# The MLP's down projection as seven Strassen products, interleaved with the gate and value products

## The chip, the cores and the metric

The kernel runs on one core of one Trainium2 chip. The metric is the device time of one execution in microseconds (us). TensorE (PE) does the matmuls, VectorE (DVE), ScalarE (ACT) and GpSimd (POOL) the work on tiles; SyncE (SP) issues most DMA transfers.

## The reference

One encoder layer over 512 tokens of 2048 features, in float32: a normalisation, an input projection, a gating unit on half of the channels and a long convolution on the other half, an output projection, and then the part that matters here, a gated MLP with 5504 hidden channels, and a final normalisation.

```
h = rms_norm(x, norm2_g[l])
gv = h @ ffn_w_up[l]
g = dwconv3(gv[..., :D_FF], ffn_dw_w[l], ffn_dw_b[l])     # three taps along the tokens
val = gv[..., D_FF:]
x = x + (jax.nn.gelu(g, approximate=False) * val) @ ffn_w_down[l]
return rms_norm(x, final_g)
```

## The kernel before

A float32 product is computed as three products in a shorter format (`mm3`): each operand is split into `hi` (a rounded copy) and `lo` (the rest), and hi·hi, lo·hi and hi·lo are summed in PSUM. Weights stream in *units* of 128x1024 (512 KB): `plan` lists them in the order of use, `load_raw` issues the load on SP's queue into one of three buffers `raw`, ACT casts it to `hi`, DVE subtracts to get `lo` (`exact_pair`), and `next_unit` keeps splits two units and loads three units ahead of the matmuls. So the order of `plan` sets the order of the work on all engines; there is no scheduler that changes it.

Activations are kept as [feature, token]: `h2H`/`h2L` are the split, normalised activations of 16 blocks of 128 features, `xacc` the residual. In the gate and value products weights are stationary and 512 tokens move through; the profile's names give the moving tile first (`pa<-h2H,hi`).

The 5504 hidden channels are 43 blocks of 128: ten groups of four and a last group of three. The order is: gate of a group (8 units of 24 matmuls), down of the group before (8 units, 192 matmuls, `pd`), value of the group (8 units). When a gate is done, DVE multiplies its four PSUM banks by the norm's row (`ev`, L563), ACT and DVE compute the three taps (`cv`, L567 and two multiply-adds of L574 per block), ACT the GELU, GpSimd multiplies by the row again (`gg`, L1034). When a value is done, DVE multiplies (L1048) and the result is split into `aH`/`aL`. Each finished feature block of the down product is added to `xacc` (L1071). The weights of the last group's down product are all split ahead into `lH`/`lL`; that product (`pl`, 288 matmuls with 256 tokens) ends the kernel in two halves of the tokens, each followed by its normalisation: squares, ones-matmuls for the sum over features, a power on GpSimd, a row broadcast by TensorE, and scaled outputs. The output leaves as [feature, token] and is transposed by the host.

Tiles stand in SBUF one after another in the order in which they are declared. Three small pads (`pad`) shift what follows them.

Of the kernel before, what the change touches and what calls it, by code (L numbers as in the profile page):

```python
# [31 lines left out]
NCC = CB // CC  # L32

# [9 lines left out]
def encoder_kernel(ctx: ExitStack, tc: tile.TileContext, a: dict, out: bass.AP):  # L43
# [40 lines left out]
    def plan_down(gi):  # L84
        j0, nf = groups[gi]
        for q in range(4):
            plan.extend((w_dn, j0 + k0, min(2, nf - k0), q * 512, 512) for k0 in range(0, nf, 2))

    ffn_order = []
    for gi in range(last):  # L90
        ffn_order.append(("gate", gi))
        if gi:
            ffn_order.append(("down", gi - 1))
        ffn_order.append(("value", gi))
    ffn_order += [("gate", last), ("value", last), ("down", last - 1)]
# [8 lines left out]

    on_pool = set()
# [3 lines left out]
    for kind, gi in ffn_order:  # L109
        if kind == "down":  # L110
            plan_down(gi)
        else:
            plan_proj(w_up, (0 if kind == "gate" else DFF) + groups[gi][0] * P, groups[gi][1])

    raws, split_units = {}, {}
    st_ = {"dma": 0, "split": 0, "use": 0}
# [16 lines left out]

    def dma_to(n):
        while st_["dma"] < min(n, len(plan)):
            raws[st_["dma"]] = load_raw(plan[st_["dma"]])
            st_["dma"] += 1

    def split_to(n):
        while st_["split"] < min(n, len(plan)):  # L140
            i = st_["split"]
            dma_to(i + 1)
            _, _, nk, _, n_ = plan[i]
            raw = raws.pop(i)
            hi = wp.tile([P, 2, 512], F32R, tag="hi", name="hi", bufs=3)
            lo = wp.tile([P, 2, 512], F32R, tag="lo", name="lo", bufs=3)
            if i == 0:
                for k in range(nk):
                    exact_pair(hi[:, k, :n_], lo[:, k, :n_], raw[:, k, :n_])
            else:  # L150
                eng = POOL if i in on_pool else DVE
                exact_pair(hi[:, :nk, :n_], lo[:, :nk, :n_], raw[:, :nk, :n_], eng)
            split_units[i] = (hi, lo)
            st_["split"] += 1

    def next_unit(key):
# [506 lines left out]
    pad("padu", 128, stack=left)  # L663
# [21 lines left out]
    def sgu_pieces():  # L685
# [328 lines left out]
    act, gates = {}, {}  # L1014
    turn_ = [1]

    def four(name, n=4):
        turn_[0] += 1
        return [(bank, sbank)[turn_[0] % 2](name) for _ in range(n)]


# [4 lines left out]
    def gate(gi):  # L1026
        j0, nf = groups[gi]

        def take(ps):
            gg = []  # L1030
            for f, cv in conv3(ff, ps, r2[0], fw, j0):
                g_ = ff.tile([P, L], F32, tag="gg", name="gg", bufs=5)
                ACT.activation(g_, cv, AF.Gelu)  # L1033
                POOL.tensor_tensor(g_, g_, r2[0], ALU.mult)  # L1034
                gg.append(g_)
            gates[gi] = gg

        return projA(w_up, j0 * P, nf, take, hk)

    def value(gi):  # L1040
        j0, nf = groups[gi]

        def take(ps):
            aH = ff.tile([P, 4, L], F32R, tag="aH", name="aH", bufs=2)
            aL = ff.tile([P, 4, L], F32R, tag="aL", name="aL", bufs=2)
            gg = gates.pop(gi)
            for f, o in enumerate(ps):
                DVE.tensor_tensor(gg[f], gg[f], o, ALU.mult)  # L1048
            for f in range(nf):
# [5 lines left out]
    def down(gi):
        j0, nf = groups[gi]
        aH, aL = act.pop(gi)
        for q in range(4):
            ps = four("pd")
            for k0 in range(0, nf, 2):  # L1060
                nk = min(2, nf - k0)
                hi, lo = next_unit((w_dn, j0 + k0, nk, q * 512, 512))
                for kk in range(nk):
                    k = k0 + kk
                    for f in range(4):
                        fs_ = slice(f * P, (f + 1) * P)
                        mm3(ps[f], hi[:, kk, fs_], lo[:, kk, fs_], aH[:, k, :], aL[:, k, :], k == 0, k == nf - 1)
                if k0 + nk == nf:
                    for f, o in enumerate(ps):
                        x_ = xacc[:, 4 * q + f, :]  # L1070
                        DVE.tensor_tensor(x_, x_, o, ALU.add)  # L1071
                yield


    r2 = []
    for kind, gi in ffn_order:
        if kind == "gate":
            g = gate(gi)
            if gi == 0:
                for n, _ in enumerate(g):  # L1080
                    if n == 1:
                        norm2(3)
                    if n == 9:
                        r2c = rms_col(ss2s[0], D, "r2c")
                    if n == 11:
                        r2.append(row_of(r2c, "r2"))
            else:
                drain(g)
        elif kind == "value":
            drain(value(gi))  # L1090
        elif gi < last - 1:
            drain(down(gi))
# [8 lines left out]
    lL = lp_.tile([P, nf, D], F32R, name="lL")  # L1101

    def last_weights():
        for q in range(4):
            for k0 in range(0, nf, 2):
                nk = min(2, nf - k0)
                raw = load_raw((w_dn, j0 + k0, nk, q * 512, 512))
                cs = slice(q * 512, (q + 1) * 512)
                exact_pair(lH[:, k0 : k0 + nk, cs], lL[:, k0 : k0 + nk, cs], raw[:, :nk, :])
                yield  # L1110

    lw = last_weights()
    for _ in down(last - 1):
        next(lw, None)
    drain(lw)
    aH, aL = act.pop(last)
    ov = out.rearrange("(k p) t -> p k t", p=P)
    HW = L // 2
    def scale(d, hs, row, eng):
        x_ = xacc[:, d, hs]  # L1120
        if eng is POOL:
            ACT.activation(x_, x_, AF.Copy, scale=col("final", d))
            POOL.tensor_tensor(x_, x_, row[:, :HW], ALU.mult)
        else:
            DVE.scalar_tensor_tensor(x_, x_, col("final", d), row[:, :HW], ALU.mult, ALU.mult)  # L1125
        if d < 2 or d % 2:
            e = d if d < 2 else d - 1
            SP.dma_start(ov[:, e : d + 1, hs], xacc[:, e : d + 1, hs])

    nt = HW // P  # L1130

    def rms3():

        ms_ = [sbank("ms") for _ in range(nt)]

        def add(sq, first, final):
            for t in range(nt):
                PE.matmul(
                    ms_[t][:, 0:1], sq[:, t * P : (t + 1) * P], ones[:, 0:1], start=first, stop=final
                )  # L1140

        def close():
            r = const.tile([P, NT], F32, tag="rc", name="r3c", bufs=3)
            for t in range(nt):
                DVE.tensor_scalar(r[:, t : t + 1], ms_[t][:, 0:1], 1.0 / D, EPS, ALU.mult, ALU.add)
            POOL.tensor_tensor(r[:, :nt], r[:, :nt], nhalf.broadcast_to([P, nt]), ALU.pow)
            return r

        return add, close

    for th in range(2):
        hs = slice(th * HW, (th + 1) * HW)

        accs = [lp_.tile([P, HW], F32, tag=f"ss{i}", name=f"ss{i}", bufs=2) for i in range(2)]
        sqs = []
        for d in range(KD):
            if th and d == KD - 1:
                add, close = rms3()
                add(accs[0], True, False)
                add(accs[1], False, False)  # L1160
                add(sqs.pop(0), False, False)
# [17 lines left out]
            if th and d == 4:  # L1179
                row = row_of(r3c, "r3", nt)  # L1180
# [97 lines left out]
```

## Time and profile before

| | |
|---|---|
| median of 3 runs | 2146.39 us (2145.21 to 2148.4) |
| profiled execution | 2145.88 us |
| its span | 2144.1 us |
| TensorE busy | 2117.5 us (99%) |
| VectorE busy | 1117.2 us (52%) |
| ScalarE busy | 671.7 us (31%) |
| GpSimd busy | 219.5 us (10%) |
| matmuls (recorded) | 9734 |

Busy shares are means over the span, and a busy engine need not be at its best pace. What a matmul costs is therefore read from the distance between the starts of two that follow one another, not from the duration in its row, in which neighbours overlap.

### The profile page before, as it was taken

Reading aid. Unit: us, or ns where it says so; the run is one execution under the profiler, and the core shown is the slowest. Engines: PE = TensorE matmul, PEld = TensorE weight load, DVE = VectorE, ACT = ScalarE, POOL = GpSimd, SP = SyncE. Lnnn points to the kernel's source line nnn. Section 1 sums busy time; section 2 is a strip of 40 time slices with the busy share of each in tenths; the row PEclk is TensorE's granted clock in tenths of the full one; section 3 lists DMA queues with packets and bytes.
Section 4 is the critical chain, followed back from the end, with each engine's and each line's share of the span. In section 5 each row is a group of like instructions: output and inputs, shape, how many; then the busy total and the mean of one; then the engine's idle time right before and its main releaser. Section 6 shows DMA issues by size and latency. Waiting matters only on the chain.

```text
span 2144.1 us, 23726 instructions
## 1 busy us (share of the span) xinstructions
PE 2117.5 (99%) x9734; PEld 1761.1 (82%) x9734; DVE 1117.2 (52%) x1336; ACT 671.7 (31%) x851; POOL 219.5 (10%) x147
## 2 busy tenths in 40 slices
PE   8999999999999999999999999999999999999997
PEld 6888888888888888888888888888888888888887
DVE  6872675447888744435343363533635345353455
ACT  6443542223543323222221222212222122222233
POOL 0330310100004410001010010100101000010004
PEclk9999999999999999999999999999999999999998
DMA  8434233333233333333333333333333333332332
GB/s 290 142 117 134 80 88 98 99 120 126 84 104 128 118 91 96 99 99 98 89 98 100 97 99 99 98 98 94 94 98 98 98 94 103 94 94 86 104 115 79
DMA packets 114632, 227.29 MB, mean 106 GB/s; under 512 B 7163, under 2 KB 18619, under 8 KB 112732
## 3 DMA queue, kind: packets, MB, share of 16 engines
q1 hardware_dynamic: 109184, 215.69, 32.6%
q10 hardware_dynamic: 5340, 10.10, 1.4%
q8 instruction: 76, 1.25, 0.3%
q14 instruction: 32, 0.26, 0.0%
HBM read 217.37 MB, written 8.39 MB: 105 GB/s over the span
## 4 chain that ended last, share of the span: by engine, by line
PE 90%; DVE 6%; ACT 1%; issue 1%; DMA 1%; POOL 0%; ACTq 0%; SPq 0%; DVEq 0%
PE pa L172 19%; PE pa L170 19%; PE pa L171 19%; PE pd L171 7%; PE pd L172 7%; PE pd L170 7%; PE po L171 2%; PE po L172 2%; PE po L170 2%; PE pv L170 1%; PE pv L172 1%; PE pv L171 1%; DVE ev L561 1%; DVE lo L132 1%; DVE xacc L1125 1%
## 5 line engine op out<-in xcount | busy, mean ns | idle before, releaser
L132 DVE TENSOR_TENSOR lo<-raw,hi 128x1024 fp32r<-128x1024 f32 (+2 forms) x369 | 459.4, 1247 | 842.4 <-ACT hi L131 837.1
L131 ACT CAST hi<-raw 128x1024 fp32r<-128x1024 f32 (+2 forms) x369 | 382.5, 1037 | 1097.0 <-PE pa L171 708.5
L170 PE MATMUL pa<-h2H,hi 128*128 128x512 f32 x1376 | 535.6, 389 | 0.0
L172 PE MATMUL pa<-h2H,lo 128*128 128x512 f32 x1376 | 535.4, 389 | 0.0
L171 PE MATMUL pa<-h2L,hi 128*128 128x512 f32 x1376 | 535.4, 389 | 0.0
L171 PEld LDWEIGHTS pa<-h2L,hi 128*128 128x128 f32 x1376 | 258.4, 188 | 53.6
L172 PEld LDWEIGHTS pa<-h2H,lo 128*128 128x128 f32 x1376 | 258.4, 188 | 53.6
L170 PEld LDWEIGHTS pa<-h2H,hi 128*128 128x128 f32 x1376 | 258.4, 188 | 53.4
L172 PE MATMUL pd<-aH,lo 128*128 128x512 f32 x640 | 249.0, 389 | 0.0
L170 PE MATMUL pd<-aH,hi 128*128 128x512 f32 x640 | 249.0, 389 | 0.0
L171 PE MATMUL pd<-aL,hi 128*128 128x512 f32 x640 | 249.0, 389 | 0.0
L170 PE MATMUL pa<-hH,hi 128*128 128x512 f32 x512 | 202.4, 395 | 2.6 <-DVE ev L561 1.5
L172 PE MATMUL pa<-hH,lo 128*128 128x512 f32 x512 | 200.3, 392 | 1.4 <-DVE lo L132 1.4
L171 PE MATMUL pa<-hL,hi 128*128 128x512 f32 x512 | 200.5, 392 | 0.0
L1034 POOL TENSOR_TENSOR gg<-gg,r 128x512 f32<-128x512 f32 x43 | 73.0, 1700 | 1203.2 <-ACT gg L1033 1203.2
L170 PEld LDWEIGHTS pd<-aH,hi 128*128 128x128 f32 x640 | 120.2, 188 | 25.0
L172 PEld LDWEIGHTS pd<-aH,lo 128*128 128x128 f32 x640 | 120.2, 188 | 24.9
L171 PEld LDWEIGHTS pd<-aL,hi 128*128 128x128 f32 x640 | 120.2, 188 | 24.9
L1071 DVE TENSOR_TENSOR xacc<-xacc,pd 128x512 f32<-128x512 f32 x160 | 106.0, 683 | 39.9 <-PE pd L172 39.9
L170 PEld LDWEIGHTS pa<-hH,hi 128*128 128x128 f32 x512 | 96.8, 189 | 28.5 <-DVE ev L561 4.6
L172 PEld LDWEIGHTS pa<-hH,lo 128*128 128x128 f32 x512 | 96.6, 189 | 23.1 <-DVE lo L132 2.7
L171 PEld LDWEIGHTS pa<-hL,hi 128*128 128x128 f32 x512 | 96.8, 189 | 19.0
(241 smaller groups left out, 2157.0 us busy)
## 6 DMA issues: line engine op xcount, KB each, us to landing
raw<-in_ffn_w_up SPq DMA_DIRECT2D x160, 512.0 KB, 3.7
raw<-in_ffn_w_down SPq DMA_DIRECT2D x84, 512.0 KB, 3.6
raw<-in_w_in SPq DMA_DIRECT2D x79, 512.0 KB, 3.7
raw<-in_w_out SPq DMA_DIRECT2D x32, 512.0 KB, 3.7
raw<-in_ffn_w_up SPq DMA_DIRECT2D x16, 384.0 KB, 3.2
xn<-in_xN ACTq DMA_DIRECT2D x8, 512.0 KB, 4.8
khat_d<-kh SPq DMA_DIRECT2D x4, 1024.0 KB, 4.4
kh<-khat_d SPq DMA_DIRECT2D x4, 1024.0 KB, 4.8
```

The lines of the kernel that those rows point to most:

```text
L131: ACT.copy(hi, src)
L132: eng.tensor_tensor(lo, src, f32(hi), ALU.subtract)
L170: PE.matmul(o, ah, bh, start=start, stop=False)
L171: PE.matmul(o, ah, bl, start=False, stop=False)
L172: PE.matmul(o, al, bh, start=False, stop=stop)
L561: DVE.tensor_tensor(eo(e), pairs(o), pairs(r), ALU.mult)
L1034: POOL.tensor_tensor(g_, g_, r2[0], ALU.mult)
L1071: DVE.tensor_tensor(x_, x_, o, ALU.add)
L1125: DVE.scalar_tensor_tensor(x_, x_, col("final", d), row[:, :HW], ALU.mult, ALU.mult)
```

## The change

The down product of a group is computed by a scheme of Strassen's with seven products of half size in place of eight. The group's activations (512 hidden channels by 512 tokens) and each half of the output columns are cut into quarters; sums and differences of the quarters are formed on DVE, for the weights in place in their load buffers (`sraw`, 4 buffers), for the activations in three pieces per group (`operands`). A unit S0 to S13 is one of seven products for one of two column halves: 12 matmuls (`sa`, `se`, `sc`, `sg` by PSUM chain), in which now the weights move and the activations are stationary. Chains are read by DVE while they are still being summed (`read=True`), since several outputs contain the same partial sums (`shared` collects one of them over all groups).

The units are spread: G0 G1 G2 S0 G3 S1 G4 S2 G5 S3 G6 S4 G7 S5 S6 V0 S7 V1 S8 V2 S9 V3 S10 V4 S11 V5 V6 V7 S12 S13, where G and V are the gate and value units of a group and S those of the group before. The conv's work on a finished gate is cut into one piece per unit (`piece`), results are taken from PSUM behind the next unit's preparation (`flush`, `posts`).

`xacc` is turned to [token, feature] on TensorE during the first gate (`turn_x`, 16 blocks of four 128x128 transposes). The last group is 144 matmuls with 512 columns, and each of four token tiles is normalised by itself: ACT squares and sums a row, DVE multiplies by `grow` (final_g broadcast by a 1 MB load), and ACT and DVE scale; outputs leave on SP's and ACT's queues.

```diff
+SUMS = (
+    ("11", None, None), ("12", "12", "11"), ("22", None, None), ("22", "22", "12"),
+    ("11", "22", "11"), ("21", None, None), ("21", "21", "22"),
+)
...
+    for gi in range(len(groups)):
+        S = [("S", gi - 1, i // 7, i % 7) for i in range(14)] if gi else []
+        G, V = ([("R", kind, gi, k0) for k0 in range(0, KD, 2)] for kind in ("gate", "value"))
+        ffn_order += G[:3]
+        for i in range(5):
+            ffn_order += S[i : i + 1] + G[3 + i : 4 + i]
+        ffn_order += S[5:7]
+        late = 2 if gi == last else 0
+        for i in range(5 - late):
+            ffn_order += V[i : i + 1] + S[7 + i : 8 + i]
+        ffn_order += V[5 - late :] + S[12 - late :]
+    ffn_order += [("L", k0, q) for q in range(4) for k0 in range(0, groups[last][1], 2)]
...
+                into, of, less = SUMS[u]
+                raws[i] = sraws[gi, dp, into]
+                if of:
+                    DVE.tensor_tensor(raws[i], sraws[gi, dp, of], sraws[gi, dp, less], ALU.subtract)
...
+    def conv_piece(gi, f):
+
+        w0, w1, w2_, b = (col(*n(groups[gi][0] + f)) for n in fw)
+        e, d = gg[gi][:, f, :], tmp[f % 2]
+        ACT.activation(d, e, AF.Identity, bias=b, scale=w1)
+        DVE.scalar_tensor_tensor(d[:, 1:L], e[:, : L - 1], w0, d[:, 1:L], ALU.mult, ALU.add)
+        DVE.scalar_tensor_tensor(d[:, : L - 1], e[:, 1:L], w2_, d[:, : L - 1], ALU.mult, ALU.add)
+        ACT.activation(e, d, AF.Gelu)
+        POOL.tensor_tensor(e, e, r2[0], ALU.mult)
...
+    CHAIN = "aeeacgc"
...
+    def down_out(gi, dp, u, tp):
+        o = chains[dp, CHAIN[u]][tp]
+        if u == 3:
+            sh = shared[:, tp, dp, :]
...
+        else:
+            t, q = ((tp, dp), (tp + 2, dp + 2), (tp, dp + 2), None, (tp + 2, dp + 2), (tp, dp), (tp + 2, dp))[u]
+            add_to(t, q, as_out(o))
...
+        hi, lo = next_unit(e, flush)
+        for tp in range(2):
+            ts_ = slice(tp * P, (tp + 1) * P)
+            for k in range(2):
+                mm3(
+                    chains[dp, CHAIN[u]][tp], H[:, u, k, ts_], Lo[:, u, k, ts_], hi[:, k, :], lo[:, k, :],
+                    k == 0 and u not in (2, 3, 6), k == 1, True,
+                )
+            posts.append(lambda tp=tp: down_out(gi, dp, u, tp))
...
+    ssf = const.tile([P, NT, 4], F32, name="ssf")
...
+        o = ps_of.pop(("last", t, q))
+        x_ = fin[t][q]
+        DVE.tensor_tensor(as_out(x_), out_tile(t, q), as_out(o), ALU.add)
+        ACT.activation(tmp[q % 2], x_, AF.Square, accum_out=ssf[:, t, q : q + 1])
+        DVE.tensor_tensor(x_, x_, grow[0][:, q * 512 : (q + 1) * 512], ALU.mult)
...
+            if q % 2:
+                ACT.activation(x_, x_, AF.Copy, scale=r[:, 0:1])
+            else:
+                DVE.tensor_scalar(x_, x_, r[:, 0:1], None, ALU.mult)
+            (ACT if q % 2 else SP).dma_start(out[t * P : (t + 1) * P, q * 512 : (q + 1) * 512], x_)
```

Two of the three pads go (`padu`, 128 B, and `pady`, 384 B), and the new tile `ssf` (64 B) stands among the first. This moves the tiles on the left side of SBUF; those on the right stay. Start addresses in the two built programs, modulo 256 bytes:

| tiles | before | after |
|---|---|---|
| `hi`, `lo` (weights) | 128 | 192 |
| `hH`, `hL`, `h2H`, `h2L` (activations of the input, gate and value products) | 128 | 128 |
| `yh`, `ylo` (output projection, first half) | 128 | 192 |
| `ybH`, `ybL` (output projection, second half) | 0 | 192 |
| `aH`, `aL` (activations of the down product) | 128 | 192 |
| `lH`, `lL` and the last group's activations | 128 | 128 |

How the order on VectorE changes where a gate ends, inside the MLP. Before (`ev` are the gate's banks times the row, `cv` the conv, `lo` the splits, `xacc` the down product's sums):

```order
L563 TENSOR_TENSOR ev<-pa,r_5817 128x512 x3
L574 SCALAR_TENSOR_TENSOR cv<-ev,cols,cv 128x511
L563 TENSOR_TENSOR ev<-pa,r_5817 128x512
L574 SCALAR_TENSOR_TENSOR cv<-ev,cols,cv 128x511 x2
L132 TENSOR_TENSOR lo<-raw,hi 128x1024
L574 SCALAR_TENSOR_TENSOR cv<-ev,cols,cv 128x511 x5
L132 TENSOR_TENSOR lo<-raw,hi 128x1024
L1071 TENSOR_TENSOR xacc<-xacc,pd 128x512 x4
```

After (`gg` stands for `ev`, `tmp` for `cv`; `sg` and `sc` are Strassen chains; `lo<-sraw` splits a Strassen unit, `lo<-raw` a value unit):

```order
L1118 TENSOR_TENSOR gg<-pa,r_5854 128x512 x3
L1110 SCALAR_TENSOR_TENSOR tmp_5856<-gg,cols,tmp_5856 128x511
L1118 TENSOR_TENSOR gg<-pa,r_5854 128x512
L144 TENSOR_TENSOR lo<-raw,hi 128x1024
L1111 SCALAR_TENSOR_TENSOR tmp_5856<-gg,cols,tmp_5856 128x511
L1192 TENSOR_TENSOR xacc<-xacc,sg 128x4x128 x2
L144 TENSOR_TENSOR lo<-sraw,hi 128x1024
L1110 SCALAR_TENSOR_TENSOR tmp_5857<-gg,cols,tmp_5857 128x511
L1192 TENSOR_TENSOR xacc<-xacc,sc 128x4x128
L1111 SCALAR_TENSOR_TENSOR tmp_5857<-gg,cols,tmp_5857 128x511
L1192 TENSOR_TENSOR xacc<-xacc,sc 128x4x128
L144 TENSOR_TENSOR lo<-raw,hi 128x1024
```

All eight multiply-adds of the conv stood with one split between them; now they are spread over four units, with splits and sums of Strassen chains between.

The order on VectorE where the last group begins, behind the last value product. Before (`aL` splits the last group's activations, `lL` its weights, `lo` and `xacc` belong to the down product before it):

```order
L1048 TENSOR_TENSOR gg<-gg,pa 128x512 x3
L132 TENSOR_TENSOR aL<-gg,aH 128x512
L132 TENSOR_TENSOR lo<-raw,hi 128x1024
L132 TENSOR_TENSOR aL<-gg,aH 128x512 x2
L132 TENSOR_TENSOR lL<-raw,lH 128x2x512
L132 TENSOR_TENSOR lo<-raw,hi 128x1024
L132 TENSOR_TENSOR lL<-raw,lH 128x512
L1071 TENSOR_TENSOR xacc<-xacc,pd 128x512 x4
L132 TENSOR_TENSOR lo<-raw,hi 128x1024
L132 TENSOR_TENSOR lL<-raw,lH 128x2x512
L132 TENSOR_TENSOR lo<-raw,hi 128x1024
L132 TENSOR_TENSOR lL<-raw,lH 128x512
```

After (`laL` the last group's activations, `shared` the collected sums, `lL` the split weights, `fin` the outputs):

```order
L144 TENSOR_TENSOR laL<-gg,laH 128x512 x3
L144 TENSOR_TENSOR lo<-sraw,hi 128x1024
L1192 TENSOR_TENSOR xacc<-xacc,shared 128x4x128
L1192 TENSOR_TENSOR xacc<-xacc,sc 128x4x128 x2
L144 TENSOR_TENSOR lL<-raw,lH 128x2x512
L1192 TENSOR_TENSOR xacc<-xacc,shared 128x4x128
L1192 TENSOR_TENSOR xacc<-xacc,sg 128x4x128 x2
L144 TENSOR_TENSOR lL<-raw,lH 128x512
L1192 TENSOR_TENSOR xacc<-xacc,shared 128x4x128
L1192 TENSOR_TENSOR xacc<-xacc,sc 128x4x128 x2
L144 TENSOR_TENSOR lL<-raw,lH 128x2x512
L1192 TENSOR_TENSOR xacc<-xacc,shared 128x4x128 x3
```

The splits of the last group's weights, which before were spread over the down product ahead of it, stand among the last Strassen sums now.

## Rows read from the trace of the kernel before

**Rows 1.** The page: busy time by engine; TensorE's clock in 40 slices.
```profile
PE 2117.5 (99%) x9734; PEld 1761.1 (82%) x9734; DVE 1117.2 (52%) x1336; ACT 671.7 (31%) x851; POOL 219.5 (10%) x147
...
PEclk9999999999999999999999999999999999999998
```
**Rows 2.** Windows in the MLP: PE, PEld, DVE, ACT, POOL busy; PE clock; DMA.
```profile
1100.00:1600.00 500.00, 500.00 (x2208) 414.18 (x2207) 218.64 (x236) 126.34 (x141) 27.28 (x16) 1.00 0.33 97
1110.00:1122.00 12.00, 12.00 (x55) 9.94 (x54) 11.93 (x13) 6.96 (x10) 5.25 (x4) 1.00 0.14 44
```
**Rows 3.** Timeline of TensorE (start, duration): into the last group, and its end.
```profile
2088.85 0.39 PE L172 MATMUL pd<-aH,lo 128*128 128x512 f32 x1
2089.08 0.28 PE L170 MATMUL pl<-aH,lH 128*128 128x256 f32 x1
...
2127.63 0.42 PE L172 MATMUL pl<-aH,lL 128*128 128x256 f32 x1
```
**Rows 4.** Timeline of TensorE around a block of eight transposes.
```profile
498.09 1.04 PE L832 MATMUL ut<-ident,u 128*128 128x128 f32 x8
498.89 0.47 PE L170 MATMUL po<-yh,hi 128*128 128x512 f32 x1
499.20 0.39 PE L171 MATMUL po<-ylo,hi 128*128 128x512 f32 x1
...
500.82 0.40 PE L172 MATMUL po<-yh,lo 128*128 128x512 f32 x1
```
**Rows 5.** Timeline of TensorE: two stretches of seven matmuls, first and eighth of each.
```profile
660.54 0.39 PE L170 MATMUL po<-ybH,hi 128*128 128x512 f32 x1
...
662.17 0.39 PE L171 MATMUL po<-ybL,hi 128*128 128x512 f32 x1
...
1200.09 0.39 PE L172 MATMUL pa<-h2H,lo 128*128 128x512 f32 x1
...
1201.68 0.39 PE L170 MATMUL pa<-h2H,hi 128*128 128x512 f32 x1
```
**Rows 6.** Groups by line and form: count, busy us, mean ns of one, idle before.
```profile
L170 PE MATMUL pa<-h2H,hi 128*128 128x512 f32 x1376 | 535.6, 389 | 0.0
...
L132 DVE TENSOR_TENSOR lo<-raw,hi 128x1024 fp32r<-128x1024 f32 x351 | 442.3, 1262 | 804.9 <-ACT hi L131 799.6 <-PE mr L251 5.2
...
L1071 DVE TENSOR_TENSOR xacc<-xacc,pd 128x512 f32<-128x512 f32 x160 | 106.0, 683 | 39.9 <-PE pd L172 39.9
...
L170 PE MATMUL pa<-hH,hi 128*128 128x512 f32 x512 | 202.4, 395 | 2.6 <-DVE ev L561 1.5 <-ACT hi L131 1.0
...
L172 PE MATMUL pa<-hH,lo 128*128 128x512 f32 x512 | 200.3, 392 | 1.4 <-DVE lo L132 1.4
...
L170 PE MATMUL po<-ybH,hi 128*128 128x512 f32 x128 | 50.6, 395 | 0.0
...
L131 ACT CAST aH<-gg 128x512 fp32r<-128x512 f32 x43 | 25.6, 618 | 37.2 <-DVE gg L1048 36.6
...
L860 DVE TENSOR_TENSOR U<-G,kh 128x1024 f32<-128x1024 f32 x4 | 4.9, 1217 | 0.0
```
**Rows 7.** Timeline behind the last matmul: GpSimd's power, VectorE's scaling.
```profile
2130.68 0.71 POOL L1146 TENSOR_TENSOR r3c<-r3c,nhalf 128x2 f32<-128x2 f32 x1 [5.95 <-DVE r3c L1145]
...
2133.10 6.87 DVE L1125 SCALAR_TENSOR_TENSOR xacc<-xacc,cols,r 128x256 f32<-128x256 f32 x11 [2.50 <-ACT r L253]
```
**Rows 8.** Timeline of VectorE behind a gate: the conv's multiply-adds.
```profile
1111.27 1.40 DVE L574 SCALAR_TENSOR_TENSOR cv<-ev,cols,cv 128x511 f32<-128x511 f32 x2
...
1113.72 6.94 DVE L574 SCALAR_TENSOR_TENSOR cv<-ev,cols,cv 128x511 f32<-128x511 f32 x5
```
**Rows 9.** Timeline of GpSimd and VectorE at 702 us.
```profile
701.47 3.87 POOL L261 TENSOR_TENSOR ss<-ss,sq 128x512 f32<-128x512 f32 x2
...
701.86 2.31 DVE L132 TENSOR_TENSOR lo<-raw,hi 128x1024 fp32r<-128x1024 f32 x1
```
**Rows 10.** DMA issues by line: count, KB each, us to landing.
```profile
raw<-in_ffn_w_down SPq DMA_DIRECT2D x84, 512.0 KB, 3.6
```

More of the change, by code (lines that the diff above doesn't have):

```diff
@@ L108, in encoder_kernel @@
             plan.extend((w_out, half * 8 + k0, 2, q * 512, 512) for k0 in range(0, 8, 2))
-    for kind, gi in ffn_order:
-        if kind == "down":
-            plan_down(gi)
+    for e in ffn_order:
+        if e[0] == "R":
+            _, kind, gi, k0 = e
+            j0, nf = groups[gi]
+            plan.append((w_up, k0, 2, (0 if kind == "gate" else DFF) + j0 * P, nf * P))
         else:
-            plan_proj(w_up, (0 if kind == "gate" else DFF) + groups[gi][0] * P, groups[gi][1])
+            plan.append(e)
     raws, split_units = {}, {}
-    st_ = {"dma": 0, "split": 0, "use": 0}
+    st_ = {"dma": 0, "pre": 0, "split": 0, "use": 0}
     def load_raw(key):
@@ L661, in encoder_kernel @@
     fs.close()
-    pad("padu", 128, stack=left)
     yps.append(pool("y", stack=left))
@@ L1013, in encoder_kernel, with flush, piece @@
     fw = (lambda i: ("fw", i), lambda i: ("fw", NFF + i), lambda i: ("fw", 2 * NFF + i), lambda i: ("fb", i))
[L1014 to L1019, printed above, removed]
+    r2, sets = [], {}
+    shared = ff.tile([P, 2, 2, 512], F32, name="shared")
+    special["raw"] = lambda: ff.tile([P, 2, 512], F32, tag="sraw", name="sraw", bufs=4)
+    posts, pieces = [], []
+    def flush():
+        while posts:
+            posts.pop(0)()
+    def piece():
+        if pieces:
+            pieces.pop(0)()
     def hk(k):
@@ L1055, in down @@
[L1055 to L1072, printed above, removed]
@@ L1075, in encoder_kernel, with out_tile @@
[L1075 to L1078, printed above, removed]
-            if gi == 0:
[L1080 to L1086, printed above, removed]
-            else:
[L1088 to L1092, printed above, removed]
+    def out_tile(t, q):
+        return xacc[:, 4 * q : 4 * q + 4, t * P : (t + 1) * P]
@@ new lines, in gate_out, with value_out @@
+    def gate_out(gi):
+        gg[gi] = ff.tile([P, 4, L], F32, tag="gg", name="gg", bufs=1)
+        for f, o in enumerate(ps_of.pop(("gate", gi))):
+            DVE.tensor_tensor(gg[gi][:, f, :], o, r2[0], ALU.mult)
+            pieces.append(lambda f=f: conv_piece(gi, f))
+    def value_out(gi):
+        assert not pieces
+        g = gg[gi]
+        for f, o in enumerate(ps_of.pop(("value", gi))):
+            DVE.tensor_tensor(g[:, f, :], g[:, f, :], o, ALU.mult)
+        if gi < last:
+            pieces.extend(operands(gi))
@@ new lines, in regular @@
+    def regular(e, hook=None):
+        _, kind, gi, k0 = e
+        j0, nf = groups[gi]
+        if k0 == 0:
+            new = sbank if kind == "value" and gi == 0 else bank
+            ps_of[kind, gi] = [new("pa") for _ in range(nf)]
+        ps = ps_of[kind, gi]
+        hi, lo = next_unit((w_up, k0, 2, (0 if kind == "gate" else DFF) + j0 * P, nf * P), flush)
+        for kk in range(2):
+            k = k0 + kk
+            for f in range(nf):
+                fs_ = slice(f * P, (f + 1) * P)
+                mm3(ps[f], hi[:, kk, fs_], lo[:, kk, fs_], *hk(k), k == 0, k == KD - 1)
+            if hook:
+                hook(k)
+        if k0 == KD - 2:
+            posts.append(lambda: (gate_out if kind == "gate" else value_out)(gi))
@@ new lines, in first_hook @@
+    def first_hook(k):
+        if k == 0:
+            norm2(3)
+        if k == 8:
+            rows.append(rms_col(ss2s[0], D, "r2c"))
+        if k == 10:
+            r2.append(row_of(rows[0], "r2"))
+            tmp.append(const.tile([P, L], F32, tag="acc", name="tmp0", bufs=1))
+            tmp.append(const.tile([P, L], F32, tag="rb", name="tmp1", bufs=2))
+        for j in (k - 1, 15 if k == 15 else -1):
+            if j >= 0:
+                turn_x(j)
+    rows = []
+    units = iter(ffn_order)
@@ L1096, in encoder_kernel @@
+    for e in units:
+        if e[0] == "S":
+            strassen(e)
+        else:
+            regular(e, first_hook if e[1:3] == ("gate", 0) else None)
+        piece()
+        if e == ("R", "value", last, KD - 2):
+            break
     a2s.close()
@@ L1101, in encoder_kernel @@
     lL = lp_.tile([P, nf, D], F32R, name="lL")
-    def last_weights():
-        for q in range(4):
[L1105 to L1149, printed above, removed]
@@ L1185, in encoder_kernel, with last_pair @@
-    for i, sq in enumerate(sqs):
-        add(sq, False, i == len(sqs) - 1)
-    r3c = close()
-    row = row_of(r3c, "r3", HW // P)
-    for d in range(KD):
-        scale(d, slice(HW, L), row, POOL if d % 3 == 2 else DVE)
+    aH = lp_.tile([P, nf, L], F32R, name="laH")
+    aL = lp_.tile([P, nf, L], F32R, name="laL")
+    ssf = const.tile([P, NT, 4], F32, name="ssf")
+    def last_pair(k0, q):
+        nk = min(2, nf - k0)
+        cs = slice(q * 512, (q + 1) * 512)
+        return lH[:, k0 : k0 + nk, cs], lL[:, k0 : k0 + nk, cs], nk
@@ new lines, in encoder_kernel, with last_operands @@
+    special["last"] = last_pair
+    def last_operands():
+        g = gg.pop(last)
+        for f in range(nf):
+            exact_pair(aH[:, f, :], aL[:, f, :], g[:, f, :])
+        grow.append(ff.tile([P, D], F32, tag="gg", name="grow", bufs=1))
+        SP.dma_start(grow[0], a["final_g"].partition_broadcast(P))
+    grow, fin = [], {}
+    for e in units:
+        if e[0] == "L":
+            break
+        strassen(e)
+        if "last" in special and e == ("S", last - 1, 1, 4):
+            last_operands()
+        piece()
@@ new lines, in last_out @@
+    def last_out(t, q):
+        if q == 0:
+            if t < 2:
+                w = ff.tile([P, D], F32, tag=("aH", "aL")[t], name="fin", bufs=1)
+                fin[t] = [w[:, i * 512 : (i + 1) * 512] for i in range(4)]
+            else:
+                ws = [special["raw"]() for _ in range(2)]
+                fin[t] = [ws[i // 2][:, i % 2, :] for i in range(4)]
+        o = ps_of.pop(("last", t, q))
[3 more added lines that the diff above has]
+        DVE.tensor_tensor(x_, x_, grow[0][:, q * 512 : (q + 1) * 512], ALU.mult)
@@ new lines, in encoder_kernel @@
+    for q in range(4):
+        for k0 in range(0, nf, 2):
+            next_unit(("L", k0, q), flush)
+            while pieces:
+                piece()
+            for k in range(k0, min(k0 + 2, nf)):
+                for t in range(2):
+                    last_mm(t, q, k)
+        posts.extend(lambda t=t, q=q: last_out(t, q) for t in range(2))
+    for t in range(2, NT):
+        for q in range(4):
+            for k in range(nf):
+                last_mm(t, q, k)
+            flush()
+            last_out(t, q)
+            if t == 2 and q % 2:
+                leave(q // 2)
+            elif t == 3 and q == 1:
+                leave(2)
@@ L1191, in encoder_kernel @@
+    leave(3)
     tail.close()
```

206 lines of the change are left out of this document (121 added, 85 removed).

## The prediction

> **What bounds the kernel now.** I read the page first: TensorE is busy for 2117.5 of 2144.1 us, at the upper of its two clock levels in nearly every slice, VectorE for 1117.2 [rows 1]. Then the windows: between 1100 and 1600 us, inside the gated MLP, TensorE is busy for all 500.00 us with 2208 matmuls, and in the twelve microseconds in which VectorE has the least room (11.93 of 12.00 busy, GpSimd 5.25) it still starts 55 [rows 2]. So the MLP costs its matmuls and nothing else: 500.00/2208 = 0.2264 us for one of N=512. Last I read the timeline where a product changes shape and behind the last matmul [rows 3, 4, 7]: there alone TensorE is held up by anything else. A change here is worth matmuls taken away, plus what it does to the pace of those left, plus the end.
>
> **The sum**, against the profiled execution's 2145.88 us, 0.5 under the median shown.
>
> 1. Down products. Ten groups of four blocks now take 4 x 4 x 4 x 3 = 192 matmuls each; fourteen units of 12 make 168. 240 fewer at 0.2264: -54.3.
>
> 2. The last group. From its first matmul (2089.08) to the end of its last (2127.63 + 0.42) it takes 38.97 us for 288 of N=256 [rows 3]. Now it is 144 of N=512, 32.6: -6.4. Against that stands VectorE: from the end of the last value product to half of this stage the order gives it two gate products, two splits, sums, seven pieces of 128x512 for the operands and `shared`, twelve posts, eight splits of `lL` and thirteen operations on `fin`, by the durations of [rows 6] (a `fin` operation and a `gg` product like `xacc`, 0.68) about 33 us, beside 10.9 (four Strassen units) + 16.3 (72 matmuls) = 27.2 on TensorE. 5.8 too much; splits run two units ahead, 4.1 us of matmuls, so some 2 us are waited for (bounds 0 and 6): -4.4 in all.
>
> 3. Turning `xacc`. Sixteen blocks of four 128x128 transposes in the first gate. The eight of [rows 4] hold the next matmul back 0.80 us; its successor starts 0.31 after it, not 0.23, and the next seven run at (500.82-499.20)/7 = 0.2314. So four cost 0.40 + 0.08 and some 0.05 of slower pace: 16 x 0.53 = +8.4. ScalarE's copies back lie in its idle three quarters [rows 2].
>
> 4. The end. From the end of the last matmul, 2128.05, to 2144.1 are 16.0 us: ones-matmuls and the power until 2131.4 (3.3), its row broadcast by 2133.1 (1.7), 6.87 of scaling until 2140.0, then 4.1 of transfers [rows 3, 7]. Now one token tile is left: add 0.68, square 0.62, reduce and scale 0.3, power 0.71, four scalings on two engines 1.4, hops 0.3, transfer 4.1: 8.1. -7.9; each price but hops is a row of [rows 6, 7], the squares priced as the cast of that size. With the power at twice its price, -7.2.
>
> That is -58.2: 2087.7 if the remaining matmuls keep their pace.
>
> 5. The pace. It depends on something that the diff does not name. `po<-ybH/ybL` takes 1.63 us for seven matmuls (0.2324 each), `pa<-h2H/h2L` 1.59 (0.2267) [rows 5]: same shape, same number of columns, the engine never waiting in either. What differs is where the two tiles stand: at yb the moving tile starts at 0 and the weights at 128 (mod 256 bytes); at h2 both stand at 128. In the changed kernel the removed pads and a 64 B tile shift everything on the left: `hi` and `lo` to 192, while `h2H/h2L` and `hH/hL` stay at 128. The pairs of all gate and value products are then 64 off, those of the Strassen units (192 and 192), of the last group (128 and 128) and of yb equal. No row of before has a pair 64 off. Bounds: nothing but the gain at yb, 384 x 5.7 ns (0.2324 less 0.2267) = -2.2; or all 4128 gate and value matmuls at yb's pace, +23.5, the 1920 of the input projections up by 3 ns (two of their lines average 392 and 395 ns, against 389 at h2 and 395 at yb [rows 6]), +5.8, and the 1680 Strassen matmuls drawn along between them, +9.6. 64 is as far from 0 as from 128, so I take halfway for the pairs that are 64 off and nothing for the others: 11.8 + 2.9 - 2.2 = +12.5.
>
> 2087.7 + 12.5 = 2100.2, as a median **2101**.
>
> A rule speaks against this step. The Trainium skill ("TensorE: Matmul & The Clock Gate", Part 2, "Step-by-step: what each phase is for") says that TensorE reads moving operand and weights through two independent ports, so that loading weights takes nothing from a running matmul. By that no pair of addresses could matter and the sum would stay at 2088. The trace disagrees as far as yb's 0.2324 goes; it does not say whether 64 B are enough.
>
> **What I cost at nothing, and what hides it.**
> - Forming weights: six subtractions of 128x1024 per group (1.22 by the nearest row, `U`), 28 posts where 16 stood (0.68), 14 splits for 16, operand pieces. VectorE's share of a group goes from 218.64/500 = 44% to some two thirds. It hides as long as each split is done before its unit.
> - The tight place is the end of a gate, shown by the order. Take as zero the start of the Strassen unit behind the eighth gate unit. Three `gg` are done by 0.35 (their chains end one after the other). Then up to the split of the second value unit: four multiply-adds at 0.70, one `gg`, four posts and three splits, 2.8 + 0.7 + 2.7 + 3.8 = 10.0: done at 10.4, wanted at 13.6 (three Strassen units of 2.72 and one value unit of 5.43). Margin 3 us.
> - Chains of PSUM that VectorE reads while they are still being summed: between two uses of a chain lies a unit of 5.43 us nearly everywhere, a post takes 0.68.
> - Loads: the bytes of `w_down` are the same, 512 KB land in 3.6 us [rows 10], and the four quarters are asked for ahead of the units that use them, with 97 GB/s in use [rows 2].
>
> **Rivals.**
> A. The pace doesn't change: 64 B do not matter, as the port rule has it. 2087.7, or 2085.5 where yb gets faster: 2086 to 2088. For it: the pace at 128 against 128 is the same in a quiet stretch and beside a busy VectorE and GpSimd [rows 2], so it is not easily disturbed; one pair alone is slow. Against: that pair is slow without exception.
> B. The full loss. 2087.7 + 23.5 + 5.8 - 2.2 = 2114.8, with the Strassen units drawn along 2124.4: 2115 to 2125. For it: transposes show that a disturbed pace takes a dozen matmuls to come back [rows 4], the length of one Strassen unit.
> C. Slower. Multiply-adds at the gate's end cost 0.70 alone and 1.39 beside GpSimd's product [rows 8], and a split beside GpSimd took 2.31 instead of 1.26 [rows 9]. If all eight multiply-adds of the burst and five splits fall so, its work to the split of the third value unit grows from 17.0 to 17.0 + 5.5 + 5.3 = 27.8, wanted at 21.7: TensorE waits 6.1 us per group, ten times: 2101 + 61 = 2162. It makes the kernel slower from (2145.9 - 2100.2)/10 = 4.6 us per group on. For it: GpSimd's products are spread out now, one per unit, right among the splits. Against: in the stretch of [rows 2] GpSimd works 5.25 of 12 us, so about half the burst can be beside it, and that half (about 5 us more, 3 hidden) costs 2 per group, 20 in all and 2121.
> D. The units do not save: a wait between Strassen units (chain or operand not ready) of 2.3 us per unit would eat the 240 matmuls; nothing in the trace has a wait of this kind, since TensorE is idle nowhere in [rows 2].
>
> **Numbers.** Halfway 0.42 (2092 to 2112); A 0.28; B, or C's small form, 0.23; C in full or D 0.05; 0.02 for an end that gives back more than it takes. The range is 2083 to 2128: from A with a cheaper end to B with the stalls of step 2 at their bound. 0.2% is 4 us, what runs of this kernel (2145.2 to 2148.4) can tell from none: faster 0.92, same 0.02, slower 0.06.
>
> **What would show it.** Step 1: `s*` matmuls 1680, no idle time of TensorE in the MLP. Step 5: matmuls started in 500 us of the MLP: 2208 means A, about 2185 halfway, 2165 to 2152 B; and 0.2267 for yb. Step 3: 0.53 us per block. Step 4: 8 us behind the last matmul. C: idle time of TensorE with `lo` as its releaser, behind each gate. Wrong in kind would be a pace that differs between Strassen and gate units the other way round, or idle TensorE in each group.

## The result, and the profile after

The changed kernel takes 2121.76 us (2121.65 to 2122.01) against 2145.81 for the kernel before, beside it on the same chip: ratio 0.9886, 95% interval 0.9869 to 0.9903. The forecast was 2101 with a range of 2083 to 2128. So the time lies in the range and on the side that was forecast, but at the place of rival B (2115 to 2125), and nearly half of the likeliest gain is missing: 24.1 of 44.9 us came. The profiled execution has a span of 2120.0 us, 24.1 less than before, and that difference is what has to be accounted for.

The page first: busy time by engine and TensorE's clock in 40 slices, to be held against [rows 1].

```profile
PE 2097.7 (99%) x9374; PEld 1703.6 (80%) x9374; DVE 1376.4 (65%) x1655; ACT 757.2 (36%) x954; POOL 217.9 (10%) x124
...
PEclk9999999999999999999999999999999999999999
```

TensorE is as full and as fast clocked as before; VectorE works 1376.4 us in place of 1117.2. The windows, in the columns of [rows 2]:

```profile
1100.00:1600.00 500.00, 500.00 (x2160) 403.97 (x2159) 323.55 (x368) 160.43 (x178) 35.01 (x16) 1.00 0.33 100
1400.00:1900.00 500.00, 500.00 (x2159) 403.93 (x2158) 316.75 (x358) 155.44 (x172) 32.44 (x15) 1.00 0.33 99
```

TensorE is still busy for all 500 us, but starts 2160 matmuls where 2208 stood: 0.2315 us each. The forecast had named 2165 to 2152 as rival B's sign. And TensorE waits for nothing there. In the list of TensorE's waits (what was waited for, total us, times, longest), up to the last group nothing belongs to the MLP; the longest ones lie in the front of the kernel, where they were before:

```profile
PE hp L358 <- DMA zw<-in_zw: 4.0, 1, 4.0
PE iv L224 <- ACT sH L143: 2.2, 3, 1.1
PE fw L225 <- DVE kL L144: 1.6, 1, 1.6
PE pa L224 <- DVE ev L615: 1.2, 4, 0.3
```

So the missing time is no wait. It is the pace of each matmul, and it differs by product. TensorE's timeline in three places; the first two answer to [rows 5], the third is the Strassen unit behind a gate:

```profile
660.54 0.39 PE L224 MATMUL po<-ybH,hi 128*128 128x512 f32 x1
...
662.13 0.39 PE L225 MATMUL po<-ybL,hi 128*128 128x512 f32 x1
```
```profile
1194.87 0.39 PE L224 MATMUL pa<-h2H,hi 128*128 128x512 f32 x1
...
1196.50 0.39 PE L225 MATMUL pa<-h2L,hi 128*128 128x512 f32 x1
```
```profile
1134.41 0.39 PE L224 MATMUL sg<-hi,aH 128*128 128x512 f32 x1
...
1135.79 0.39 PE L224 MATMUL sg<-hi,aH 128*128 128x512 f32 x1
...
1137.15 0.39 PE L224 MATMUL sc<-hi,aH 128*128 128x512 f32 x1
...
1139.87 0.39 PE L224 MATMUL pa<-h2H,hi 128*128 128x512 f32 x1
```

`po<-ybH/ybL` now takes 1.59 us for seven matmuls (0.2271), where it took 1.63. `pa<-h2H/h2L` takes 1.63 (0.2329), where it took 1.59. The two have changed places, and so have their start addresses: the two tiles of yb are now equal modulo 256, those of h2 are 64 B apart. A Strassen unit needs six matmuls to settle (1134.41 to 1135.79: 0.230 each), then runs at 0.2267 (1135.79 to 1137.15, six). Averages over all matmuls of a product, from start to start, leaving out gaps over 260 ns:

| product | before | after |
|---|---|---|
| `pa<-h` (input projections) | 227.4 ns | 233.3 |
| `pv` (input projections, weights moving) | 227.3 | 229.3 |
| `po<-yb` | 232.5 | 227.0 |
| `pa<-h2` (gate and value) | 226.7 | 233.3 |
| `pd`, then Strassen units | 226.7 | 228.1 |

### The profile page after: what moved, and what is told of

It is laid out like the page before. It is cut to its first block, busy times and chain, and to the rows that moved or that the text cites. A ratio compares the mean times of both kernels' runs of the same rounds, so it can differ in the third digit from the quotient of the medians.

```text
span 2120.0 us, 23470 instructions
## 1 busy us (share of the span) xinstructions
PE 2097.7 (99%) x9374; PEld 1703.6 (80%) x9374; DVE 1376.4 (65%) x1655; ACT 757.2 (36%) x954; POOL 217.9 (10%) x124
## 4 chain that ended last, share of the span: by engine, by line
PE 92%; DVE 5%; ACT 1%; issue 1%; DMA 1%; SPq 0%; ACTq 0%; POOLq 0%; DVEq 0%
PE pa L226 20%; PE pa L224 20%; PE pa L225 20%; PE po L224 2%; PE po L225 2%; PE po L226 2%; PE se L225 2%; PE se L224 2%; PE se L226 2%; PE sa L225 2%; PE sa L224 2%; PE sa L226 2%; PE sc L225 2%; PE sc L224 2%; PE sc L226 2%; PE pv L224 1%
## 5 line engine op out<-in xcount | busy, mean ns | idle before, releaser
L144 DVE TENSOR_TENSOR lo<-raw,hi 128x1024 fp32r<-128x1024 f32 (+2 forms) x289 | 359.6, 1247 | 279.5 <-ACT hi L143 279.1
L143 ACT CAST hi<-raw 128x1024 fp32r<-128x1024 f32 (+2 forms) x289 | 298.6, 1033 | 554.4 <-PE pa L225 266.1
L144 DVE TENSOR_TENSOR lo<-sraw,hi 128x1024 fp32r<-128x1024 f32 x140 | 171.6, 1226 | 336.0 <-ACT hi L143 335.9
L143 ACT CAST hi<-sraw 128x1024 fp32r<-128x1024 f32 x140 | 147.0, 1050 | 490.7 <-PE pa L225 419.1
L1113 POOL TENSOR_TENSOR gg<-gg,r 128x512 f32<-128x512 f32 x43 | 91.1, 2130 | 1193.6 <-ACT gg L1112 1193.6
L180 DVE TENSOR_TENSOR sraw<-sraw 128x1024 f32<-128x1024 f32 x80 | 98.8, 1235 | 18.2 <-DMA sraw<-in_ffn_w_down 17.9
L225 PE MATMUL sa<-lo,aH 128*128 128x512 f32 x160 | 62.7, 392 | 0.0
L225 PE MATMUL se<-lo,aH 128*128 128x512 f32 x160 | 62.7, 392 | 0.0
L224 PE MATMUL sc<-hi,aH 128*128 128x512 f32 x160 | 62.4, 390 | 0.1
L225 PE MATMUL sc<-lo,aH 128*128 128x512 f32 x160 | 62.5, 391 | 0.0
```

Of the source, the lines that this page charges most:

```text
L143: ACT.copy(hi, src)
L144: eng.tensor_tensor(lo, src, f32(hi), ALU.subtract)
L180: DVE.tensor_tensor(raws[i], sraws[gi, dp, of], sraws[gi, dp, less], ALU.subtract)
L224: PE.matmul(o, ah, bh, start=start, stop=False, skip_group_check=read)
L225: PE.matmul(o, ah, bl, start=False, stop=False, skip_group_check=read)
L1113: POOL.tensor_tensor(e, e, r2[0], ALU.mult)
```

## The experiments

Four theories stood at this point. *Distance*: the pace depends on how far the start addresses of the moving and the stationary tile are apart, modulo 256 B. *Work*: TensorE is slowed by what VectorE, ScalarE and the reads of unfinished PSUM chains now do beside it. *Place*: it is the weights' own address (192) that is slow. *Burst* (rival C): VectorE's work behind a gate decides, hidden so far.

**Equal pairs.** One number of the changed kernel:

```diff
-    pad("padr", 96, "right")
+    pad("padr", 32, "right")
```

> The changed kernel with one number edited: the pad on the right side is 32 B in place of 96, which moves h2H, hH and the last group's tiles by 64 B, so that all pairs of a moving and a stationary tile are equal modulo 256. Theory (distance of the two start addresses): gate and value matmuls go from 233.3 to 226.7 ns (4128 x 6.6 = 27.2 us), the input projections from 233.3 to 227.4 (1536 x 5.9 = 9.1), pv 384 x 2 = 0.8, and Strassen units lose their settling (1680 x 1.4 = 2.3): 2121.8 - 39.4 = 2082. Rival (work): the pace is slower because VectorE, ScalarE and reads of PSUM are busier between Strassen units; nothing of that changes, 2122. Rival (place of the weights): hi and lo still start at 192, 2122.

2085.46 us (2085.40 to 2085.52); ratio to the kernel before 0.9717, interval 0.9702 to 0.9731. This is the distance theory, within 3.5 us of its number; of these, 2.6 lie in the front of the kernel, which gives back 7.3 us (`pa<-h2` starts at 714.48, not 721.74) and not 9.9. Work and place are out, since all instructions and the weights' addresses are as in the changed kernel. Window and timeline of this run:

```profile
1400.00:1900.00 500.00, 500.00 (x2207) 414.01 (x2207) 327.50 (x372) 162.69 (x180) 35.41 (x16) 1.00 0.33 101
```
```profile
1199.91 0.39 PE L224 MATMUL pa<-h2H,hi 128*128 128x512 f32 x1
...
1201.50 0.39 PE L225 MATMUL pa<-h2L,hi 128*128 128x512 f32 x1
```

2207 matmuls in the 500 us, VectorE as busy as in the changed kernel, and seven `pa` again in 1.59 us. Strassen units run at 226.7 without settling. This version beats both kernels: 60.7 us under the one before, 36.3 under the changed one.

**The other way round.** The kernel before, with an unused tile of the size of `ssf`, and no Strassen:

```diff
     const = pool("const")
+    const.tile([P, 16], F32, name="shift")
```

> The kernel before with nothing but an unused 64 B tile among the first ones: hi and lo (and aH, yh) move by 64 B, h2H and hH stay. No Strassen, no new work on any engine. Theory: gate and value at 233.3 (+27.2), input projections (+9.1), pv (+0.8), pd unchanged (its pairs stay equal), the last group unknown (64 off, 256 columns): 2146 + 37 = 2183. Rival (work): no change, 2146.

2181.09 us; ratio 1.0163 (1.0146 to 1.0180). 64 unused bytes cost 35 us.

```profile
1400.00:1900.00 500.00, 500.00 (x2165) 405.11 (x2165) 209.46 (x226) 120.66 (x133) 23.28 (x14) 1.00 0.32 95
```
```profile
1200.15 0.39 PE L171 MATMUL pa<-h2H,hi 128*128 128x512 f32 x1
...
1201.78 0.39 PE L172 MATMUL pa<-h2L,hi 128*128 128x512 f32 x1
```

Seven `pa` take 1.63 us, while `pd`, whose two tiles moved together, keeps 226.8 ns in the same kernel.

**Other distances.** The same pad at 64, 160, 224, 256 and 288 B.

> The same pad at 64 B: the pairs of gate and value products and of the input projections are 32 B apart instead of 64. Theory: slower than at 0; if the loss grows with the distance, half of 39 us is left, 2102; if any distance breaks the pace, 2122. Rivals of work or of the weights' place: 2122.

2124.19 us. A distance of 32 costs as much as one of 64; from 32 to 64 the loss does not grow with the distance.

> The same pad at 160 B: these pairs are 128 B apart, as yb's were in the kernel before. Theory: yb's pace there, 232.5 ns: 0.8 ns less than at 64 for 5664 matmuls, 2117. Rivals of work or of the weights' place: 2122.

2121.07 us, where the theory had 2117: at this distance `pa<-h2` ran at 233.0 ns and not at yb's 232.5, and `pv` became slower, 232.4 for 229.3.

> The changed kernel with the right pad at 224 B: in the gate, value and input products the weights (stationary) now start 192 B behind the moving tile, which modulo 256 is 64 B ahead of it; in pv, where weights move, it is the other way round, 64 behind. Theory with a sign: pv ran at 229.3 ns in the changed kernel with just this distance of 192, so pa should run at 229.3 and pv at 233.3: 2085.5 + 5664 x 2.4 = 13.6 + 384 x 6 = 2.3 + about 1 of settling: 2102. Theory without a sign, in which pv is less slow because its moving tile is the weights: pa at 233.3, pv at 229.3, 2122.

2106.44 us, nearer to the 2102 of a distance with a sign than to 2122: `pa` ran at 229.4 and `pv` at 233.3, just as `pv` at 192 and `pa` at 64 had in the changed kernel. The 4 us above the forecast lie in the Strassen units: it had allowed about 1 us for settling, but their average is 230.2 ns here, 5.9 us in all.

> The changed kernel with the right pad at 256 B: weights of the gate, value and input products stand 224 B behind the moving tile (32 ahead of it, modulo 256), those of pv 32 behind. Theory with a sign, from the run at 32 B, where pv had just this distance of 224 and ran at 233.3 ns: pa at 233.3 as well, 2124. If the loss shrinks evenly from 192 (229.4 ns) towards 256: 228 ns, 2093.

2125.82 us: what `pv` showed at 224 in the run at 32 B holds for `pa`.

> The right pad at 288 B: the two tiles stand 256 B apart. If only the distance modulo 256 counts: 226.7 ns and 2085.5, as with equal pairs. If the period is longer (512): a slower pace, 2105 to 2124.

2087.22 us (2086.05 and 2088.39), at the paces of the equal pairs: 256 B are as good as 0, so the period is 256 B.

The windows of these five runs between 1400 and 1900 us, each in its own fence, in the order 32, 128, 192, 224, 256:

```profile
1400.00:1900.00 500.00, 500.00 (x2158) 404.94 (x2157) 316.97 (x359) 155.69 (x173) 32.92 (x15) 1.00 0.32 98
```
```profile
1400.00:1900.00 500.00, 500.00 (x2162) 405.45 (x2161) 317.38 (x359) 155.69 (x172) 32.73 (x15) 1.00 0.32 99
```
```profile
1400.00:1900.00 500.00, 500.00 (x2178) 408.94 (x2177) 322.97 (x366) 160.38 (x177) 30.47 (x14) 1.00 0.31 100
```
```profile
1400.00:1900.00 500.00, 500.00 (x2155) 403.83 (x2154) 316.40 (x359) 155.58 (x172) 32.96 (x15) 1.00 0.32 98
```
```profile
1400.00:1900.00 500.00, 500.00 (x2208) 414.01 (x2207) 327.20 (x373) 162.89 (x180) 35.37 (x16) 1.00 0.33 101
```

In all of them TensorE is busy for 500.00 us at full clock, with 2158, 2162, 2178, 2155 and 2208 matmuls. Paces, by the distance of the stationary tile behind the moving one. The last column has the Strassen units of the kernel in which `pa<-h2` has this distance; their own two tiles are equal modulo 256 in every row:

| distance mod 256 | `pa<-h2` | `pv` | Strassen units beside `pa<-h2` |
|---|---|---|---|
| 0 | 226.8 ns | 227.3 | 226.7 |
| 32 | 233.4 | 233.2 | 228.4 |
| 64 | 233.3 | 233.3 | 228.1 |
| 128 | 233.0 | 232.4 | 227.7 |
| 192 | 229.4 | 229.3 | 230.2 |
| 224 | 233.4 | 233.3 | 229.2 |

Weights are stationary in `pa` and moving in `pv`, and both columns agree to 0.6 ns: it is the distance and not which tile holds what. An equal pair is not enough, though: the last column shows that it also depends on the matmuls before it. Behind gate and value matmuls at a distance of 64 a Strassen unit is at 226.7 ns from its sixth matmul on, behind those at 192 only from its eleventh, so there it is on average slower than the matmuls around it (230.2 against 229.4).

**yb in the kernel before.**

```diff
-    pad("padu", 128, stack=left)
+    pad("padu", 256, stack=left)
...
-                yp.tile([P, 96], F32, name="pady")
+                yp.tile([P, 64], F32, name="pady")
```

> The kernel before with its pads at 256 and 256 B in place of 128 and 384, which moves ybH and ybL alone, from 128 B off the weights to an equal place modulo 256. Theory: 384 matmuls from 232.5 to 227.0 ns, 2.1 us: 2144.3 against 2146.4, with all else as before. If yb is slow for what runs beside it (the last blocks of the norm, GpSimd's squares): 2146.4 and 232.5.

2143.77 us against 2146.20; ratio 0.9985 (0.9975 to 0.9995). `po<-yb` ran at 227.0 ns:

```profile
660.48 0.39 PE L172 MATMUL po<-ybH,lo 128*128 128x512 f32 x1
...
662.07 0.39 PE L170 MATMUL po<-ybH,hi 128*128 128x512 f32 x1
```

Seven in 1.59 us, where [rows 5] have 1.63.

**VectorE's margin.** The kernel with equal pairs, with 2 and with 6 operations more in each conv piece:

```diff
+        for _ in range(2):
+            DVE.tensor_tensor(d, d, d, ALU.max)
         ACT.activation(e, d, AF.Gelu)
```

> The kernel with equal pairs, with two more operations of 128x512 on VectorE (0.6 us each, a maximum of a tile with itself, which changes no value) in each of the four conv pieces behind a gate: 4.8 us per group. In the changed kernel the tightest splits end 2.6 to 3.5 us before their first matmul (the first two value units behind the conv pieces). By the margin at the burst, 1.2 to 1.8 us fall before the first value unit and 3.6 before the second: at most some tenths per group are waited for, 2085 to 2092. By the share of VectorE's time (two thirds): 2085.5.

2089.93 us, 4.5 more: behind each of nine gates one matmul starts some 0.34 us late and the next 0.11, 4.1 in all.

> The same with six more operations per piece, 14.4 us per group. By the margin at the burst (about 3 us there, and some 2 more that a wait of TensorE itself wins): 8 to 11 us of waiting in each of eleven groups, 2170 to 2205. By VectorE's share, which stays under 80%: 2085.5.

2190.51 us, 105 more, within the margin's 2170 to 2205, but in nine groups and not eleven. The waits of TensorE in the two runs, within the MLP (total us, times, longest):

```profile
PE pa L226 <- DVE lo L144: 1.8, 9, 0.4
```
```profile
PE pa L226 <- DVE lo L144: 72.5, 9, 8.1
```

72.5 of the 105 us are these waits; the others lie behind them (last section). That the time fell within the forecast is partly luck: 2085.46 and 72.5 of waits make 2158, below its range, and the forecast had nothing of what lies behind them. VectorE's windows in the two runs:

```profile
1100.00:1600.00 500.00, 499.31 (x2199) 412.22 (x2198) 349.17 (x403) 161.45 (x179) 27.62 (x16) 1.00 0.31 101
```
```profile
1100.00:1600.00 500.00, 467.55 (x2007) 383.31 (x2006) 362.80 (x435) 149.57 (x164) 28.62 (x16) 0.96 0.28 91
```

VectorE was busy for 349 and 363 of 500 us, so its share does not decide, the burst does. The margin that the forecast worked out was real, and small: 4.8 us per group is just over the edge.

**No turning of `xacc`.**

```diff
         for j in (k - 1, 15 if k == 15 else -1):
-            if j >= 0:
-                turn_x(j)
+            pass
```

> The kernel with equal pairs, without the 16 blocks of four transposes of xacc in the first gate and ScalarE's copies back (the residual is left unturned, so this leaves out a part of the computation). By the trace of the changed kernel a block holds the next matmul back by 0.354 us, and that one's successor by 0.318 - 0.233 = 0.085: 16 x 0.44 = 7.0, so 2078.5. By the forecast's 0.53 per block: 2077.1. If ScalarE's copies delayed splits as well, less than that.

2078.35 us: the transposes cost 7.1 us, and the 7.0 read from TensorE's timeline account for it.

## Why the prediction came out as it did

**Step 1, down products: right.** 1680 matmuls stand for 1920, no wait came with them (rival D is out), and with equal pairs they run at 226.7 ns: -54.3.

**Step 2, the last group: right in size (-4.4 forecast).** In the changed kernel the last Strassen matmul starts at 2077.41, and its successors, nearly all `pl`, end at 2110.87; with 0.72 us for two `pl` that come earlier this is 33.9 for 38.97, -5.0. The forecast had 2 us of waits; six gaps of over 260 ns cost 1.1 in all.

**Step 3, transposes: somewhat too dear (+8.4).** The timeline of TensorE around one block, against [rows 4]:

```profile
727.34 0.60 PE L1096 MATMUL xt<-ident,xacc 128*128 128x128 f32 x4
727.69 0.48 PE L224 MATMUL pa<-h2H,hi 128*128 128x512 f32 x1
728.01 0.40 PE L225 MATMUL pa<-h2L,hi 128*128 128x512 f32 x1
728.25 0.39 PE L226 MATMUL pa<-h2H,lo 128*128 128x512 f32 x1
```

The next matmul starts 0.35 us after the block, its successor 0.32 after that, then 0.24. 16 blocks are 7.0; the run without them gave 7.1. The forecast had 0.40 and 0.08, and 0.05 for a slower pace behind them. Half of what eight transposes cost was too much for four, and the slower pace does not show.

**Step 4, the end: -7.9 forecast, -6.9 measured.** From the end of the last matmul, 2110.87, to 2120.0 are 9.1 us. The chain of waits there:

```profile
2110.91 0.70 DVE sraw L1299
...
2111.63 0.73 ACT tmp L1300 x2
...
2112.39 0.69 DVE sraw L1301
...
2113.48 0.58 POOLq L1426
...
2114.71 0.71 ACT sraw L1318
```

Square and multiplication stand one after the other, since both use the tile (ACT reads it, then VectorE overwrites it); the forecast had them side by side. That is 0.7 of the 1.0 us which was missing. The last transfer adds 0.5, 4.6 us from the end of the last scaling for the 4.1 of before, and the other steps together give 0.2 back.

**Step 5, the pace: this step failed, by its size.** "64 is as far from 0 as from 128, so I take halfway" gave +12.5. Measured in the changed kernel: 4128 x 6.6 ns = 27.2 for gate and value, 1680 x 1.4 = 2.4 for the settling of Strassen units, and 5.4 for the front (`pa<-h2` starts at 721.74, not 716.31; 7.8 by the paces; the rest is mostly shorter gaps in the front, 1.6 of it in the input projections): +35.0. The four other steps come to -59.2, and -59.2 + 35.0 = -24.2 is the measured -24.1. The mechanism, the distance of the two start addresses, was the forecast's; the assumption that a loss interpolates between two distances was not in any row. Only a distance of 0 has the full pace: 32, 64, 128 and 224 cost 6.2 to 6.6 ns in `pa<-h2`, 192 costs 2.6, and no order by size is in it. What I had called rival B's bound, yb's 5.7 ns, was not even the worst case: the distance of 64 costs 6.6. And the 3 ns for the input projections, as their bound, came from durations of rows (392 and 395 ns), in which neighbours overlap; from start to start `pa<-h` lost 5.9 (227.4 to 233.3) and `pv` 2.0. The result is in the range because rival B set its upper end, not because the likeliest sum was near.

That Strassen units would be *drawn along* (9.6 of rival B's 37) was too much for this kernel: they settle within six matmuls, not the dozen of [rows 4], and lose 2.4 us. Behind gate matmuls at a distance of 192 they need nearly that dozen.

Rival A had the pace unchanged: out for the changed kernel, but it is what the kernel with equal pairs does. Its lower end, 2085.5, where yb gets faster, is the 2085.46 measured there. So the sum of steps 1 to 4 was right to about a microsecond, in part by luck: in the changed kernel the errors of steps 2, 3 and 4 are -0.6, -1.4 and +1.0 and partly cancel.

**The rule on two ports.** The Trainium skill ("TensorE: Matmul & The Clock Gate", Part 2, "Step-by-step: what each phase is for") has the moving operand and the weights read through independent ports, so that a load takes nothing from a running matmul. From this the forecast concluded that no pad could change the time. The runs disagree with that conclusion: 64 B of pad on one side are worth 36 us, with the same instructions. Whether the two reads meet somewhere is not shown. The rows show that the loads do not become longer (188 ns on average at h2 before, 187 after), while the matmuls do (389 and 395). Where that arises, and why a distance of 192 costs 2.6 ns and its neighbours 6.6, stays open.

**Rival C, the burst: rightly given little, but not far off.** Splits and matmuls of the first two value units behind a gate, in the changed kernel (VectorE, then TensorE; a unit's `lo` is wanted from its third matmul on):

```profile
1135.77 1.22 DVE L144 TENSOR_TENSOR lo<-raw,hi 128x1024 fp32r<-128x1024 f32 x1
...
1139.89 1.79 DVE L1110 SCALAR_TENSOR_TENSOR tmp<-gg,cols,tmp 128x511 f32<-128x511 f32 x1
...
1143.46 1.21 DVE L144 TENSOR_TENSOR lo<-raw,hi 128x1024 fp32r<-128x1024 f32 x1
```
```profile
1140.33 0.39 PE L226 MATMUL pa<-h2H,lo 128*128 128x512 f32 x1
...
1148.21 0.39 PE L224 MATMUL pa<-h2H,hi 128*128 128x512 f32 x1
```

The first value unit's split ends at 1136.99, 2.9 us ahead of its unit at 1139.87. The forecast had worked out the second unit's: split done at 10.4, unit at 13.6, a margin of 3. From the same zero, 1134.41, that split ends at 10.3 and its unit starts at 13.8, a margin of 3.5. The multiply-add at 1139.89 took 1.79 beside GpSimd, those at 1136.90 and 1142.20, with no product beside them, 0.75 and 0.74. Over the kernel, against 1091 ns for a multiply-add before and 1700 for GpSimd's product (groups by line: count, busy us, mean ns, idle before):

```profile
L180 DVE TENSOR_TENSOR sraw<-sraw 128x1024 f32<-128x1024 f32 x80 | 98.8, 1235 | 18.2 <-DMA sraw<-in_ffn_w_down 17.9
...
L1113 POOL TENSOR_TENSOR gg<-gg,r 128x512 f32<-128x512 f32 x43 | 91.1, 2130 | 1193.6 <-ACT gg L1112 1193.6
...
L1110 DVE SCALAR_TENSOR_TENSOR tmp<-gg,cols,tmp 128x511 f32<-128x511 f32 x43 | 51.0, 1205 | 0.2 <-ACT tmp L1109 0.2
...
L1111 DVE SCALAR_TENSOR_TENSOR tmp<-gg,cols,tmp 128x511 f32<-128x511 f32 x43 | 32.0, 763 | 0.1
```

GpSimd's product became longer, 2130 ns, and of the two multiply-adds one takes 1205, the other 763: the collision is there, in part of the places, as supposed, but inside the margin: TensorE waited for none of it. The subtraction of weights took 1235 for the 1217 of its nearest row.

## What to carry to other kernels

Read the pace of matmuls from start to start and product by product, before looking for waits: here a fully busy engine lost 3% of its pace, and no view of waits showed it. A change that adds or removes a small tile moves everything allocated behind it; print the start addresses of moving and stationary tiles before and after, and make them equal modulo 256 B with a pad. A product whose own two tiles are equal can still be slowed by an unequal one before it, for three to ten matmuls here. And when an unknown lies between two known cases, ask whether it can be in between at all, before taking the middle.

## What the runs showed of the hardware

The dependence on the distance itself, with its sign and its period of 256 B (the table above), was not expected in this form. Nor was a second price of a wait. In the run with six more operations TensorE waits 8.1 us per group, and the granted clock falls (windows: PE, PEld, DVE, ACT, POOL busy, then the clock):

```profile
1150.00:1164.00 14.00, 13.95 (x62) 11.14 (x61) 14.00 (x20) 7.02 (x8) 4.42 (x2) 1.00 0.12 37
1164.00:1172.50 8.50, 0.47 (x3) 0.05 (x1) 8.50 (x13) 1.26 (x2) 1.64 (x2) 0.72 0.00 0
1172.50:1176.00 3.50, 3.48 (x8) 2.81 (x9) 3.50 (x4) 0.00 (x0) 1.09 (x1) 0.50 0.48 150
1176.00:1180.00 4.00, 4.00 (x15) 3.12 (x14) 3.49 (x4) 1.05 (x1) 0.00 (x0) 0.75 0.45 140
1180.00:1190.00 10.00, 10.00 (x46) 8.29 (x45) 5.50 (x7) 2.18 (x3) 0.00 (x0) 1.00 0.33 103
```

The clock falls during the wait (0.72 on average) and stands at 0.50 behind it (1.2 of 2.4 GHz); eight matmuls start in the next 3.5 us (0.43 us each). In the window from 1180 on it is at its upper level again. That is where most of the other 30 us of this run went: about 3 on top of each wait of 8.1.
